# Weight sums by adding transfers in the plain token-stationary groups, with all signs turned to plus

## The chip, the cores and the metric

The kernel runs on one core of a Trainium2 chip. The time is device time in microseconds (us). TensorE (PE) multiplies, VectorE (DVE) and ScalarE (ACT) do elementwise work, GpSimd (POOL) does small arithmetic and issues transfers, SyncE (SP) issues transfers. All transfers of the core, whichever engine issues them, run on sixteen DMA engines.

## The reference

One block of a streaming encoder, 512 tokens of width 2048, all in float32:

```python
h = rms_norm(x, norm_g[l])
proj = h @ w_in[l]                       # 2048 -> 15,424 columns, split 13 ways
...
conv_y = b_gate * causal_depthwise_conv(c_gate * u, conv_w[l])
o_conv = (conv_y * jax.nn.silu(conv_z)) @ w_conv_out[l]
mla_y = mla_attention(c_q, c_kv, k_rope_raw, ...)      # 16 heads, block-causal
o_mla = (mla_y * jax.nn.silu(mla_z)) @ w_mla_out[l]
mem_y = memory_attention(mem_q, mem, ...)              # 4 heads over 256 memory tokens
o_mem = (mem_y * jax.nn.silu(mem_z)) @ w_mem_out[l]
merged = (jax.nn.sigmoid(g_conv) * o_conv + jax.nn.sigmoid(g_mla) * o_mla
          + jax.nn.sigmoid(g_mem) * o_mem)
x = x + merged @ w_o[l]
```

Most of the work is large matrix products with weights that are read once from memory.

## The kernel before, in words

**Products in three passes.** Every float32 operand is cut in two parts: ACT copies the raw tile to "whi" (the upper part), and DVE subtracts that from the raw tile and writes "wlo" (`forms_of`, by way of `split`). `mm3` makes a product of three matmuls: upper × upper, upper × lower, lower × upper.

**Seven products in place of eight.** Most of the large weight products are done as two-by-two block products: the tokens in two halves, the input width in two halves (tiles E and O), the output columns in two halves. With weight blocks w00, w01, w11, w10 (first digit: half of the input width; second: half of the columns), a group computes seven products P1 to P7. Each is a weight block, or a sum of weight blocks, times an activation block or a sum of such. P1, P4 and P2 use w00, w11 and w10 as they are. P7 uses w00 with w01, P5 uses w01 with w11, P6 uses P5's sum with w00, P3 uses P6's sum with w10. The sums of activations are made once by `build_sums`; the sums of weights are made in every group by DVE, in place, in the tile "raw" that holds the loaded block, and the result is cut into whi and wlo. The seven results are combined by `t_results` or `f_results` out of the accumulation banks X, Y, Z and W (`SLOT`).

**Three kinds of group.** A *feature-stationary* group (`f_group`, six of them) holds weights in PE and streams tokens. A *token-stationary* group (`t_group`, fifteen of them) holds tokens and streams 512 weight columns. Three of the fifteen are "lead" groups, the first after a change of activations, with an order of their own (`LEAD_ORDER`). The other twelve are called plain here: four for the conv branch (w_conv), five gate groups (one of w_gmem, two of w_gconv, two of w_gmla), w_memq, and the second groups of w_mla_out and w_o. There are also direct groups (`d_group`) without block sums.

**Steps.** A token-stationary group has 28 steps, one for each product and each of four chunks c of the input width. A step is made of forms (load, weight sum, whi and wlo) and parts (12 matmuls). `run_range` writes a step's matmuls, then the next step's forms, then what is to follow the step (results, loads of gates, transposes of the conv branch). whi and wlo lie in six buffers "wf", three steps' worth; in the attention stage some lie in "w" buffers. `T_ORDER` gives the order of steps of the plain groups:

```python
T_ORDER = [(n, c) for names in (("P1", "P7"), ("P5", "P4"), ("P6",), ("P3", "P2"))
           for c in range(4) for n in names]
```

**Loads.** All weight blocks stand in one list (`to_load`), 0.5 MB each as 128 × 1024 float32. `fetch(key)` issues loads on SP's queue up to that key, and beyond it up to eight ahead while fewer than `cap` of the ten "w" buffers are taken (`wlive`). `done(key)` gives a buffer back. A plain group before loads twenty blocks: 00 and 01 by turns, then 11, then 00 once more ("00b", for P6), then 10.

**Order on the engines.** SP's instructions run in the order of the program. In two stretches (the start, and the attention heads up to the first steps after them) the order on all engines is planned ahead by the kernel's own `Player`, with a table of costs. Elsewhere the framework's planner places the instructions of PE, DVE, ACT and POOL by an estimated timeline; each engine then takes its queue in that order.

**POOL.** In the first half POOL does next to nothing. In the mla_out groups (`mla_group`) POOL loads gates ("g", by `early`) and adds results into a tensor in memory ("mdram", by `store`, a transfer with accumulate); around it are loads of attention outputs ("araw") and of the conv groups' gates and sums ("g", "m"). In the w_o groups (`out_group`) POOL loads blocks of x and ACT's queue stores the output.

**Conv transposes.** After each pair of conv groups, `conv_turn` is hooked to steps 0, 2, 4 and 6 of the next plain group: eight PE transposes, three ACT and DVE passes each over 128 × 512.

Of the kernel before, what the change touches and what calls it, by code (L numbers as in the profile page):

```python
# [261 lines left out]
def body(ctx, tc, a, out):  # L262
# [142 lines left out]
    cap, limit = [NW], [None]  # L405

    def fetch(key):
        k = place[key]
        while issued[0] < len(loads) and (issued[0] <= k or (issued[0] < min(k + AHEAD, limit[0])
                                                             and wlive[0] < cap[0])):  # L410
            kk, src = loads[issued[0]]
            issued[0] += 1
            raws[kk] = w("raw")
            nc.sync.dma_start(flat(raws[kk]), src)
        return raws[key]

    def done(key):
        del raws[key]
        w_done()

    def to_load(key, src):
        place[key] = len(loads)
        loads.append((key, src))

# [17 lines left out]
    def run_all(gen):  # L442
        for _ in gen:
# [5 lines left out]
               for c in range(2) for n in names]  # L449
    T_ORDER = [(n, c) for names in (("P1", "P7"), ("P5", "P4"), ("P6",), ("P3", "P2"))  # L450
               for c in range(4) for n in names]
# [4 lines left out]
    def f_group(src, B, results, tag):  # L456
# [7 lines left out]
        def forms(name, c):  # L464
            w00, w01, w11, w10 = ((gid, k, c) for k in ("00", "01", "11", "10"))
            if name in ("P1", "P2", "P4"):
                key = {"P1": w00, "P2": w10, "P4": w11}[name]
                r = forms_of(fetch(key))
                if name != "P1":
                    done(key)  # L470
                return r
            if name == "P7":
                src_ = q("s")
                vec.tensor_tensor(out=src_, in0=fetch(w00), in1=fetch(w01), op=ALU.subtract)
                return forms_of(src_)
            i0, i1, op = {"P5": (w01, w11, ALU.add), "P6": (w01, w00, ALU.subtract),
                          "P3": (w10, w01, ALU.subtract)}[name]
            src_ = fetch(w01)
            vec.tensor_tensor(out=src_, in0=fetch(i0), in1=fetch(i1), op=op)
# [25 lines left out]
    def t_group(src, B, results, lead=False):  # L505
        gid = count[0] = count[0] + 1
        bk = {}
        w00, w01, w11, w10 = (src[4 * i:4 * i + 4] for i in range(4))
        cs_ = ((0, 1, 2), (3,)) if lead else ((0, 1, 2, 3),)
        for cs in cs_:  # L510
            if lead:
# [3 lines left out]
            else:  # L515
                for c in cs:
                    to_load((gid, "00", c), w00[c])
                    to_load((gid, "01", c), w01[c])
        for key, ws in ((("11b", w11),) if lead else (("11", w11), ("00b", w00))) + (("10", w10),):
            for c in range(4):  # L520
                to_load((gid, key, c), ws[c])

        def forms(name, c):
            key, other, op, dead = {
                "P1": ("00", None, None, ""), "P7": ("00", "01", ALU.subtract, "00"),
                "P5": ("01", "11", ALU.add, "11" if lead else ""),
                "P4": ("11b" if lead else "11", None, None, "11b" if lead else "11"),
                "P6": ("01", "00b", ALU.subtract, "00b"), "P2": ("10", None, None, "10"),
                "P3": ("01", "10", ALU.subtract, "01")}[name]
# [73 lines left out]
    def build_sums(E, O):  # L603
# [177 lines left out]
    def f_results(consume):  # L781
# [4 lines left out]
        def results(name, bk):  # L786
# [7 lines left out]
            elif name == "P5":  # L794
                vec.tensor_tensor(out=v, in0=bk["Z"], in1=v, op=ALU.add)
            elif name == "P6":
                vec.tensor_tensor(out=u, in0=bk["W"], in1=u, op=ALU.add)
                r1 = q("r1")
# [3 lines left out]
            elif name == "P3":  # L802
                sc["r0"] = q("r0")
                vec.tensor_tensor(out=sc["r0"][:, :, HS:], in0=pair(bk["Z"]), in1=pair(u), op=ALU.add)
# [11 lines left out]
    def t_results(put, direct, early=None, add=None, own=True):  # L816
# [4 lines left out]
        def results(name, bk):  # L821
            seen.add(name)
            if name in ("P1", "P7"):
                k, slot = ("u", "X") if name == "P1" else ("v", "Y")
                sc[k] = q(k)
                for tt in range(2):
                    act.activation(sc[k][:, tt], bk[slot][tt], AF.Copy)
                if early and name == "P7":
                    early(1, 1)
            u, v = sc.get("u"), sc.get("v")  # L830
            if name == "P5":
                for tt in range(2):
                    vec.tensor_tensor(out=v[:, tt], in0=bk["Z"][tt], in1=v[:, tt], op=ALU.add)
                if add:
                    vec.tensor_tensor(out=flat(v), in0=flat(v), in1=flat(add(1, 1)), op=ALU.add)
                if early:
                    early(0, 1)
# [8 lines left out]
            if name in ("P4", "P6") and seen >= {"P4", "P6"}:  # L846
# [3 lines left out]
                if add:  # L850
                    vec.tensor_tensor(out=flat(r), in0=flat(r), in1=flat(add(0, 1)), op=ALU.add)
                    vec.tensor_tensor(out=flat(u), in0=flat(u), in1=flat(add(1, 0)), op=ALU.add)
                put(0, 1, r)
# [4 lines left out]
            if name == "P3":  # L858
                r = q("r")
                for tt in range(2):  # L860
                    vec.tensor_tensor(out=r[:, tt], in0=bk["Z"][tt], in1=u[:, tt], op=ALU.add)
                put(1, 0, r)
# [859 lines left out]
```

## Time and profile before

| | |
|---|---|
| median of 3 runs | 2101.59 us (2100.2 to 2102.88) |
| profiled execution | 2101.8 us, span 2100.0 us |
| granted TensorE clock, mean | 0.998 |
| busy: PE, DVE, ACT, POOL | 99%, 78%, 50%, 7% |
| read from memory, written | 292.61 MB, 44.17 MB |
| queue of SP (q1) | 251.92 MB, 36.9% of sixteen engines' span |
| queue of POOL (q0) | 45.57 MB, 7.2% |

Busy time is the union of an engine's instructions. A line of groups reads: source line, engine, operation, result and operands, form, count, then busy time in us, mean in ns, and the idle time of the engine ahead of these instructions with what ended it. Nearly all work is recorded under line 233, where the kernel's recorder passes instructions on, so tiles' names tell the groups apart. A line of a stage reads: from and to, length, busy time of PE, weight loads, DVE, ACT and POOL with counts, granted clock, busy share of the DMA engines, GB/s.

### The profile page before, as it was taken

What the parts mean: (1) busy time and instruction counts of PE and PEld (TensorE: products, weight loads), DVE (VectorE), ACT (ScalarE), POOL (GpSimd) and SP (SyncE); (2) the same over time, 40 slices, a digit from 0 to 9 for tenths busy, and PEclk for the clock granted to TensorE, in tenths of its full rate; (3) what the DMA queues carried; (4) which work ended last, traced back from release to release, by engine and by line L of the source; (5) the groups of instructions that cost most, each with busy time, mean ns of one, the idle gap of its engine ahead of it and who ended that gap; (6) DMA issues with size and microseconds to landing.
All of it is one profiled execution on the core that took longest, in us unless ns stands there. A gap on an engine that the chain in (4) does not pass through costs nothing.

```text
span 2100.0 us, 28564 instructions
## 1 busy us (share of the span) xinstructions
PE 2083.3 (99%) x10818; PEld 1795.1 (85%) x10818; DVE 1642.5 (78%) x2162; ACT 1057.7 (50%) x1524; POOL 150.5 (7%) x183
## 2 busy tenths in 40 slices
PE   9999999999999999999999999999999999999999
PEld 9888888887899988899888888888988888888887
DVE  6887788788777787777787787788887688867987
ACT  5544344344444445444445566576776344433543
POOL 0000000000000000000000021213221201110000
PEclk9999999999999999999999999999999999999999
DMA  7346444444533445534546664312323867675672
GB/s 261 124 161 201 134 137 144 144 134 133 188 121 125 147 131 188 173 121 151 166 144 225 208 208 153 126 64 81 111 92 106 292 221 205 207 229 176 205 238 78
DMA packets 106332, 338.66 MB, mean 161 GB/s; under 512 B 11089, under 2 KB 11617, under 8 KB 106193
## 3 DMA queue, kind: packets, MB, share of 16 engines
q1 hardware_dynamic: 71360, 251.92, 36.9%
q0 software_dynamic: 13792, 45.57, 7.2%
q10 hardware_dynamic: 21040, 39.33, 5.0%
q8 instruction: 85, 1.39, 0.3%
q14 instruction: 55, 0.44, 0.1%
HBM read 292.61 MB, written 44.17 MB: 160 GB/s over the span
## 4 chain that ended last, share of the span: by engine, by line
PE 95%; DVE 2%; ACT 1%; issue 1%; DMA 1%; POOL 0%; ACTq 0%; DVEq 0%; POOLq 0%
PE aux L233 40%; PE acc L233 33%; PE aux L237 12%; PE acc L237 10%; DVE wlo L233 0%; DMA raw<-in_w_ckv 0%; DVE cv L233 0%; DVE raw L233 0%; ACT whi L233 0%; DMA raw<-in_w_mla_out 0%; DMA raw<-in_w_memz 0%; ACT s L237 0%; DVE ss L237 0%; DVE r L233 0%; DVE s L233 0%
## 5 line engine op out<-in xcount | busy, mean ns | idle before, releaser
L233 ACT ACTIVATE whi<-raw 128x1024 fp32r<-128x1024 f32 x521 | 550.5, 1060 | 765.2 <-PE aux L233 347.6
L233 DVE TENSOR_TENSOR wlo<-raw,whi 128x1024 fp32r<-128x1024 f32 x521 | 633.6, 1222 | 285.9 <-ACT whi L233 281.7
L233 DVE TENSOR_TENSOR raw<-raw 128x1024 f32<-128x1024 f32 x258 | 315.2, 1223 | 10.3 <-DMA raw<-in_w_mla_out 3.4
L233 PE MATMUL aux<-whi,b 128*128 128x512 f32 x896 | 293.3, 389 | 1.4 <-ACT whi L233 1.4
L233 PE MATMUL aux<-whi,f 128*128 128x512 f32 x880 | 289.7, 390 | 0.0
L233 PE MATMUL acc<-whi,b 128*128 128x512 f32 x880 | 287.1, 390 | 0.8 <-ACT whi L233 0.7
L233 PEld LDWEIGHTS aux<-whi,b 128*128 128x128 f32 x896 | 168.0, 188 | 37.0 <-ACT whi L233 2.3
L233 PEld LDWEIGHTS acc<-whi,b 128*128 128x128 f32 x880 | 164.9, 188 | 35.5 <-ACT whi L233 1.6
L233 PEld LDWEIGHTS aux<-whi,f 128*128 128x128 f32 x880 | 165.0, 188 | 34.3 <-ACT E L233 0.3
L233 PE MATMUL aux<-wlo,b 128*128 128x512 f32 x448 | 174.3, 389 | 0.0
L233 PE MATMUL aux<-wlo,f 128*128 128x512 f32 x440 | 171.9, 391 | 1.0 <-DVE wlo L233 0.9
L233 PE MATMUL acc<-wlo,b 128*128 128x512 f32 x440 | 171.8, 390 | 0.7 <-DVE wlo L233 0.7
L233 PE MATMUL acc<-whi,f 128*128 128x512 f32 x448 | 140.5, 389 | 0.0
L237 DVE TENSOR_TENSOR wlo<-raw,whi 128x1024 fp32r<-128x1024 f32 (+3 forms) x92 | 99.1, 1084 | 29.2 <-ACT whi L237 24.9
L237 ACT ACTIVATE whi<-raw 128x1024 fp32r<-128x1024 f32 (+3 forms) x92 | 86.6, 951 | 63.3 <-PE acc L237 23.0
L233 PEld LDWEIGHTS aux<-wlo,f 128*128 128x128 f32 x440 | 82.6, 188 | 19.4 <-DVE wlo L233 2.2
L233 PEld LDWEIGHTS aux<-wlo,b 128*128 128x128 f32 x448 | 84.1, 188 | 17.6 <-DVE wlo L233 0.2
L233 PEld LDWEIGHTS acc<-whi,f 128*128 128x128 f32 x448 | 84.1, 188 | 17.5
L233 PEld LDWEIGHTS acc<-wlo,b 128*128 128x128 f32 x440 | 82.6, 188 | 18.1 <-DVE wlo L233 1.2
L233 PE MATMUL acc<-wlo,f 128*128 128x512 f32 x224 | 87.1, 389 | 0.0
L233 PE MATMUL acc<-whi,mT 128*128 128x512 f32 x256 | 80.8, 392 | 0.0
L233 POOL DMA_DIRECT2D mraw<-in_memT x4 | 2.2, 552 | 1082.5 <-DMA gdram<-r 1061.2
(385 smaller groups left out, 4097.4 us busy)
## 6 DMA issues: line engine op xcount, KB each, us to landing
raw<-in_w_conv SPq DMA_DIRECT2D x80, 512.0 KB, 4.1
raw<-in_w_gmem SPq DMA_DIRECT2D x44, 512.0 KB, 3.9
raw<-in_w_mla_out SPq DMA_DIRECT2D x44, 512.0 KB, 5.1
raw<-in_w_o SPq DMA_DIRECT2D x44, 512.0 KB, 4.3
raw<-in_w_gconv SPq DMA_DIRECT2D x40, 512.0 KB, 4.0
raw<-in_w_gmla SPq DMA_DIRECT2D x40, 512.0 KB, 3.9
raw<-in_w_mlaz SPq DMA_DIRECT2D x32, 512.0 KB, 4.0
raw<-in_w_mem_kv SPq DMA_DIRECT2D x32, 512.0 KB, 4.8
```

The lines of the kernel that those rows point to most:

```text
L233: return f(*args, **kw)
L237: self.player.add(self.eng, lambda: f(*args, **kw), kind, writes, reads)
```

## The change

All weight sums become plain sums. `build_sums` turns the signs of two activation sums, and `f_results` and `t_results` turn additions into subtractions to match; the number of instructions there stays the same.

In the plain groups the sums for P5, P7 and P6 are no longer made by DVE. POOL's queue issues transfers that read a weight block from memory and add it to a raw tile in SBUF:

- w11 is added onto the tile of w01 (P5's sum). `to_load` carries it as `more`; `fetch` issues it once two further loads have been issued, or at the latest when the tile is fetched.
- When P1's forms of a chunk are made, w01 is added onto the tile of w00 (P7's sum).
- When P5's forms of a chunk are made, w00 is added onto the tile of w01 (P6's sum).

P3's sum stays with DVE. The second load of w00 goes, so a plain group has 16 loads and 12 adding transfers. The steps are put in the order P1, P5, P7, then P6 and P4 by turns, then P3 and P2 by turns. P5's result is the first that is copied from its banks, and P7's comes after it. Lead and feature-stationary groups keep their sums on DVE.

```diff
+    onto = []
+
     def fetch(key):
         k = place[key]
         while issued[0] < len(loads) and (issued[0] <= k or (issued[0] < min(k + AHEAD, limit[0])
                                                              and wlive[0] < cap[0])):
-            kk, src = loads[issued[0]]
+            kk, src, more = loads[issued[0]]
             issued[0] += 1
             raws[kk] = w("raw")
             nc.sync.dma_start(flat(raws[kk]), src)
+            if more is not None:
+                onto.append((kk, issued[0], more))
+            while onto and (issued[0] >= onto[0][1] + 2):
+                add_onto()
+        while any(kk == key for kk, _, _ in onto):
+            add_onto()
         return raws[key]
+
+    def add_onto():
+        kk, _, more = onto.pop(0)
+        nc.gpsimd.dma_start(flat(raws[kk]), more, accum_op=ALU.add)
...
-    T_ORDER = [(n, c) for names in (("P1", "P7"), ("P5", "P4"), ("P6",), ("P3", "P2"))
+    T_ORDER = [(n, c) for names in (("P1",), ("P5",), ("P7",), ("P6", "P4"), ("P3", "P2"))
                for c in range(4) for n in names]
...
+        else:
+            for c in range(4):
+                to_load((gid, "00", c), w00[c])
+            for c in range(4):
+                to_load((gid, "01", c), w01[c], w11[c])
+            for key, ws in (("11", w11), ("10", w10)):
+                for c in range(4):
+                    to_load((gid, key, c), ws[c])
 
         def forms(name, c):
-            key, other, op, dead = {
-                "P1": ("00", None, None, ""), "P7": ("00", "01", ALU.subtract, "00"),
...
+            key, other, dead = {
+                "P1": ("00", None, ""), "P7": ("00", "01", "00"), "P5": ("01", "11", "11" if lead else ""),
+                "P4": ("11b" if lead else "11", None, "11b" if lead else "11"),
+                "P6": ("01", "00b", "00b" if lead else ""), "P2": ("10", None, "10"),
+                "P3": ("01", "10", "01")}[name]
             src_ = fetch((gid, key, c))
-            if other:
-                ins = (src_, fetch((gid, other, c)))
-                in0, in1 = reversed(ins) if name == "P3" else ins
-                vec.tensor_tensor(out=src_, in0=in0, in1=in1, op=op)
+            if other and (lead or name == "P3"):
+                vec.tensor_tensor(out=src_, in0=src_, in1=fetch((gid, other, c)), op=ALU.add)
             r = forms_of(src_)
+            if not lead and name in ("P1", "P5"):
+                nc.gpsimd.dma_start(flat(src_), (w01 if name == "P1" else w00)[c], accum_op=ALU.add)
             for k in dead.split():
                 done((gid, k, c))
             return r
...
-        vec.tensor_tensor(out=v[0], in0=o1, in1=e1, op=ALU.subtract)
-        vec.tensor_tensor(out=v[1], in0=v[0], in1=e0, op=ALU.add)
+        vec.tensor_tensor(out=v[0], in0=e1, in1=o1, op=ALU.subtract)
+        vec.tensor_tensor(out=v[1], in0=e0, in1=v[0], op=ALU.subtract)
         vec.tensor_tensor(out=v[2], in0=o0, in1=v[1], op=ALU.subtract)
-        vec.tensor_tensor(out=e1, in0=e1, in1=e0, op=ALU.subtract)
+        vec.tensor_tensor(out=e1, in0=e0, in1=e1, op=ALU.subtract)
...
-            if name in ("P1", "P7"):
-                k, slot = ("u", "X") if name == "P1" else ("v", "Y")
-                sc[k] = q(k)
+            if name in ("P5", "P7"):
+                n, b = (1, bk["Z"]) if name == "P5" else (0, bk["Y"])
+                if "v" not in sc:
+                    sc["v"] = q("v")
+                    for tt in range(2):
+                        act.activation(sc["v"][:, tt], b[tt], AF.Copy)
+                    if early:
+                        early(1, 1)
+                else:
+                    v = sc["v"]
+                    for tt in range(2):
+                        ins = (b[tt], v[:, tt])
+                        vec.tensor_tensor(out=v[:, tt], in0=ins[n], in1=ins[1 - n], op=ALU.subtract)
...
+            if name == "P1":
+                sc["u"] = q("u")
                 for tt in range(2):
-                    act.activation(sc[k][:, tt], bk[slot][tt], AF.Copy)
-                if early and name == "P7":
-                    early(1, 1)
+                    act.activation(sc["u"][:, tt], bk["X"][tt], AF.Copy)
...
-                    vec.tensor_tensor(out=u[:, tt], in0=bk["W"][tt], in1=u[:, tt], op=ALU.add)
+                    vec.tensor_tensor(out=u[:, tt], in0=bk["W"][tt], in1=u[:, tt], op=ALU.subtract)
```

More of the change, by code (lines that the diff above doesn't have):

```diff
@@ L419, in done, with to_load @@
         w_done()
-    def to_load(key, src):
+    def to_load(key, src, more=None):
         place[key] = len(loads)
-        loads.append((key, src))
+        loads.append((key, src, more))
     class Step:
@@ L473, in forms @@
                 src_ = q("s")
-                vec.tensor_tensor(out=src_, in0=fetch(w00), in1=fetch(w01), op=ALU.subtract)
+                vec.tensor_tensor(out=src_, in0=fetch(w00), in1=fetch(w01), op=ALU.add)
                 return forms_of(src_)
-            i0, i1, op = {"P5": (w01, w11, ALU.add), "P6": (w01, w00, ALU.subtract),
-                          "P3": (w10, w01, ALU.subtract)}[name]
             src_ = fetch(w01)
-            vec.tensor_tensor(out=src_, in0=fetch(i0), in1=fetch(i1), op=op)
+            vec.tensor_tensor(out=src_, in0=src_, in1=fetch({"P5": w11, "P6": w00, "P3": w10}[name]), op=ALU.add)
             r = forms_of(src_)
@@ L508, in t_group @@
         w00, w01, w11, w10 = (src[4 * i:4 * i + 4] for i in range(4))
-        cs_ = ((0, 1, 2), (3,)) if lead else ((0, 1, 2, 3),)
-        for cs in cs_:
-            if lead:
+        if lead:
+            for cs in ((0, 1, 2), (3,)):
                 for key, ws in (("00", w00), ("01", w01), ("11", w11), ("00b", w00)):
@@ L514, in t_group @@
                         to_load((gid, key, c), ws[c])
[L515 to L519, printed above, removed]
-            for c in range(4):
-                to_load((gid, key, c), ws[c])
-        def forms(name, c):
-            key, other, op, dead = {
-                "P1": ("00", None, None, ""), "P7": ("00", "01", ALU.subtract, "00"),
[L526 to L529, printed above, removed]
+            for key, ws in (("11b", w11), ("10", w10)):
+                for c in range(4):
+                    to_load((gid, key, c), ws[c])
+        else:
+            for c in range(4):
+                to_load((gid, "00", c), w00[c])
[3 more added lines that the diff above has]
+                for c in range(4):
+                    to_load((gid, key, c), ws[c])
+        def forms(name, c):
+            key, other, dead = {
[3 more added lines that the diff above has]
+                "P3": ("01", "10", "01")}[name]
             src_ = fetch((gid, key, c))
-            if other:
-                ins = (src_, fetch((gid, other, c)))
-                in0, in1 = reversed(ins) if name == "P3" else ins
-                vec.tensor_tensor(out=src_, in0=in0, in1=in1, op=op)
+            if other and (lead or name == "P3"):
+                vec.tensor_tensor(out=src_, in0=src_, in1=fetch((gid, other, c)), op=ALU.add)
             r = forms_of(src_)
+            if not lead and name in ("P1", "P5"):
+                nc.gpsimd.dma_start(flat(src_), (w01 if name == "P1" else w00)[c], accum_op=ALU.add)
             for k in dead.split():
@@ L794, in results @@
             elif name == "P5":
-                vec.tensor_tensor(out=v, in0=bk["Z"], in1=v, op=ALU.add)
+                vec.tensor_tensor(out=v, in0=v, in1=bk["Z"], op=ALU.subtract)
             elif name == "P6":
-                vec.tensor_tensor(out=u, in0=bk["W"], in1=u, op=ALU.add)
+                vec.tensor_tensor(out=u, in0=bk["W"], in1=u, op=ALU.subtract)
                 r1 = q("r1")
@@ L803, in results @@
                 sc["r0"] = q("r0")
-                vec.tensor_tensor(out=sc["r0"][:, :, HS:], in0=pair(bk["Z"]), in1=pair(u), op=ALU.add)
+                vec.tensor_tensor(out=sc["r0"][:, :, HS:], in0=pair(bk["Z"]), in1=pair(u), op=ALU.subtract)
             elif name == "P2":
@@ L822, in results @@
             seen.add(name)
-            if name in ("P1", "P7"):
-                k, slot = ("u", "X") if name == "P1" else ("v", "Y")
-                sc[k] = q(k)
+            if name in ("P5", "P7"):
[11 more added lines that the diff above has]
+                        vec.tensor_tensor(out=v[:, tt], in0=ins[n], in1=ins[1 - n], op=ALU.subtract)
+                    if add:
+                        vec.tensor_tensor(out=flat(v), in0=flat(v), in1=flat(add(1, 1)), op=ALU.add)
+                    if early:
+                        early(0, 1)
+            if name == "P1":
+                sc["u"] = q("u")
                 for tt in range(2):
-                    act.activation(sc[k][:, tt], bk[slot][tt], AF.Copy)
-                if early and name == "P7":
-                    early(1, 1)
+                    act.activation(sc["u"][:, tt], bk["X"][tt], AF.Copy)
             u, v = sc.get("u"), sc.get("v")
[L831 to L837, printed above, removed]
             if name == "P6":
                 for tt in range(2):
-                    vec.tensor_tensor(out=u[:, tt], in0=bk["W"][tt], in1=u[:, tt], op=ALU.add)
+                    vec.tensor_tensor(out=u[:, tt], in0=bk["W"][tt], in1=u[:, tt], op=ALU.subtract)
                 r = q("r")
@@ L851, in results @@
                     vec.tensor_tensor(out=flat(r), in0=flat(r), in1=flat(add(0, 1)), op=ALU.add)
-                    vec.tensor_tensor(out=flat(u), in0=flat(u), in1=flat(add(1, 0)), op=ALU.add)
+                    vec.tensor_tensor(out=flat(u), in0=flat(u), in1=flat(add(1, 0)), op=ALU.subtract)
                 put(0, 1, r)
@@ L860, in results @@
                 for tt in range(2):
-                    vec.tensor_tensor(out=r[:, tt], in0=bk["Z"][tt], in1=u[:, tt], op=ALU.add)
+                    vec.tensor_tensor(out=r[:, tt], in0=bk["Z"][tt], in1=u[:, tt], op=ALU.subtract)
                 put(1, 0, r)
```

## The prediction

> **What bounds the kernel now.** I read the page first (busy time, slices, chain), then the chain in order of time, then the stages one by one.
>
> ```profile
> PE 2083.3 (99%) x10818; PEld 1795.1 (85%) x10818; DVE 1642.5 (78%) x2162; ACT 1057.7 (50%) x1524; POOL 150.5 (7%) x183
> PE   9999999999999999999999999999999999999999
> PE 95%; DVE 2%; ACT 1%; issue 1%; DMA 1%; POOL 0%; ACTq 0%; DVEq 0%; POOLq 0%
> ...
> L233 PE MATMUL aux<-whi,b 128*128 128x512 f32 x896 | 293.3, 389 | 1.4 <-ACT whi L233 1.4
> ...
> 200.37 24.48 PE aux L233 x108
> 224.85 10.88 PE acc L233 x48
> ```
>
> PE is busy for 99% of the span and in every slice. A busy PE need not be at its pace, so the chain in order of time is read for that: 108 matmuls of 512 columns in 24.48 us and 48 in 10.88 us, both 226.7 ns each, although one is shown as lasting 389 ns (they overlap). One step of a token-stationary group is 12 matmuls, 2.72 us; a group of 28 steps is 76.2 us. The change leaves the number of matmuls alone, so it can win only what PE loses against that pace in the twelve plain groups. These lie, by their loads, in 193–577 (four conv groups, one gate group), 737–891, 970–1198, about 1776–1852 and at the end.
>
> ```profile
> 192.00:268.00 76.00, 76.00 (x337) 62.90 (x337) 59.24 (x55) 30.73 (x31) 0.00 (x0) 1.00 0.43 134
> 344.00:422.00 78.00, 77.43 (x346) 63.37 (x345) 65.16 (x65) 32.63 (x36) 0.00 (x0) 1.00 0.46 148
> 500.00:577.00 77.00, 74.91 (x348) 61.53 (x346) 64.78 (x66) 38.35 (x43) 0.00 (x0) 1.00 0.50 164
> 1046.00:1122.00 76.00, 76.00 (x337) 62.94 (x336) 58.59 (x54) 35.80 (x38) 1.68 (x3) 1.00 0.53 178
> 1122.00:1198.00 76.00, 75.53 (x341) 62.40 (x340) 64.85 (x72) 44.27 (x56) 3.85 (x6) 1.00 0.57 190
> 1776.00:1852.00 76.00, 76.00 (x337) 62.94 (x336) 63.92 (x60) 35.26 (x36) 12.50 (x15) 1.00 0.75 229
> ```
>
> These are single groups: length, then busy time of PE, weight loads, DVE, ACT and POOL, clock, DMA share, GB/s. Undisturbed groups have PE at 76.00 of 76.00 with DVE at 59 us (78%): DVE is not late there. Three miss 0.57, 2.09 and 0.47 us, 3.1 us together. The first two carry the conv transposes, the third the memory tokens.
>
> ```profile
> PE aux L233 <- ACT whi L233: 1.4, 2, 1.0
> PE aux L233 <- DVE wlo L233: 0.9, 2, 0.5
> PE acc L233 <- DVE wlo L233: 0.8, 2, 0.4
> PE acc L233 <- ACT whi L233: 0.7, 1, 0.7
> ...
> L233 ACT ACTIVATE whi<-raw 128x1024 fp32r<-128x1024 f32 x25 | 26.5, 1059 | 34.4 <-PE aux L233 16.7 <-PE acc L233 9.5 <-DVE raw L233 8.1
> L233 DVE TENSOR_TENSOR raw<-raw 128x1024 f32<-128x1024 f32 x14 | 17.0, 1224 | 0.2
> ```
>
> Above are PE's waits from 190 to 1200 us; below, two groups of 500–577. ACT waited there 8.1 us for a weight sum (raw<-raw) on DVE. So the loss is DVE's: the sums share it with the conv arithmetic. Two of the seven waits (0.8 us) stand where a feature-stationary group begins, which keeps its DVE sums. The other five are 3.0 us, and each hides up to 389 − 227 ns more under a modelled end: 0.8 us. The ceiling of the gain is about 3.9 us.
>
> **The change, part by part.**
>
> *DVE sums.* A plain group had 16 sums (P7, P5, P6, P3, four each); P3's four stay. 12 × 12 = 144 go.
>
> ```profile
> L233 DVE TENSOR_TENSOR raw<-raw 128x1024 f32<-128x1024 f32 x258 | 315.2, 1223 | 10.3 <-DMA raw<-in_w_mla_out 3.4
> L233 DVE TENSOR_TENSOR wlo<-raw,whi 128x1024 fp32r<-128x1024 f32 x521 | 633.6, 1222 | 285.9 <-ACT whi L233 281.7
> raw<-in_w_conv SPq DMA_DIRECT2D x80, 512.0 KB, 4.1
> g<-gdram POOLq DMA_DIRECT2D x24, 512.0 KB, 7.1
> mdram<-r POOLq DMA_DIRECT2D x8, 512.0 KB, 9.3
> ...
> L233 POOL DMA_DIRECT2D mdram<-r x8: 1187/1240/1704, 1749.6 to 1853.8; - x8
> L233 POOL DMA_DIRECT2D m<-mdram x8: 724/724/1705, 1836.8 to 1926.4; - x8
> ...
> q0 software_dynamic: 575, 1.19, 86.4%
> q1 hardware_dynamic: 150, 0.55, 20.5%
> ```
>
> 144 × 1.223 = 176 us of DVE, 14.7 us of a group's 59. Nearly all of it lay beside PE. On the path it is worth between 0 and the 3.9 us above. In the new order the first eight steps (P1, P5) have no DVE sum, and there the conv transposes fall, so I take both of those losses as gone (4 waits, 2.6 us + 0.6 hidden) and half of the third: **−3.5 us**. The wait that follows next is PE's own pace.
>
> *Transfers.* A plain group goes from 20 loads on SP's queue to 16, and gains 12 adding transfers on POOL's: −48 and +144 over the program, 96 × 0.524 MB = 50 MB more read. The trace has no adding transfer into SBUF; the nearest row is mdram<-r, which adds into DRAM: 1.2 us of POOL to issue, 9.3 us to land. The last two rows are the queues from 1778.3 to 1785.9 us, where such adds filled q0: 1.19 MB at 86.4% of 7.6 us is 181 GB/s, against 0.55 MB at 20.5%, 353 GB/s, for loads. So half a megabyte costs all sixteen engines 2.9 us when added and 1.5 us when loaded. An add into SBUF may cost as little as a load (1.5) or as much as where the slowest one landed (13.6 us, below). I take 2.9 us and 9.3 us, the same operation.
>
> *DMA time of a group.* 20 × 0.524 MB in 76 us at share 0.43 is 1.6 us each. After: 16 × 1.6 + 12 × 2.9 = 60 us, 0.80 of 76, +0.37. Gate groups with stores come to 0.53 + 0.37 = 0.90. These fit. The mla_out group comes to 0.75 + 0.37 = 1.12: it does not.
>
> *The wait that is added.* A sum now has to land before ACT and DVE cut it into whi and wlo. "fetch" and the new order give the distances in steps: the add onto 00 follows P1 c and is needed by P7 c, 8 steps or 21.8 us on; the second onto 01 follows P5 c and is needed by P6 c, 8 to 11 steps on. The first one onto 01 is the tight one: it goes out once two later loads are issued, for c = 3 with the forms of step 2, and is needed by those of step 7, 5 steps or 13.6 us on. Behind it is slack: six wf buffers hold three steps, so forms begin two steps (5.4 us) ahead of PE and take 1.06 + 1.22 us, leaving 3.1. POOL is in order: ahead of that add stand the ones onto 00 c0, 01 c2 and 00 c1, released within two steps, 1.2 us of issue apart: 3 × 2.9 us of queue, of which 3.9 us have passed. So it lands after 9.3 + 4.8 = 14.1 us, against 13.6 − 1.2 + 3.1 = 15.5. It fits with 1.4 us to spare: **0**, in eleven groups. If the landing were the 13.6 us, it would be 2.9 us late; if an add took over 3.4 us of the engines, it would begin to be.
>
> [...]
>
> *mla_out's plain group.* Here POOL also adds results into mdram and loads gates.
>
> ```profile
> 1749.60 1.25 POOL L233 DMA_DIRECT2D mdram<-r  x1 [2.69 <-DVE r L233]
> 1760.60 0.74 POOL L233 DMA_DIRECT2D g<-gdram  x1 [9.75 <-DMA mdram<-r]
> 1774.72 1.20 POOL L233 DMA_DIRECT2D mdram<-r  x1 [12.13 <-DVE r L233]
> 1776.45 1.19 POOL L233 DMA_DIRECT2D mdram<-r  x1 [0.53 <-DVE r L233]
> 1787.24 0.72 POOL L233 DMA_DIRECT2D g<-gdram  x1 [2.29 <-DMA mdram<-r]
> 1795.04 0.72 POOL L233 DMA_DIRECT2D araw<-adram  x1 [4.72 <-PE aux L233]
> ...
> 1776.00:1796.00 20.00, 20.00 (x90) 16.57 (x89) 18.25 (x17) 10.23 (x12) 4.89 (x6) 1.00 0.99 274
> 1796.00:1816.00 20.00, 20.00 (x90) 16.57 (x89) 14.99 (x14) 7.68 (x9) 0.73 (x1) 1.00 0.73 252
> ...
> DMA to landing us min/median/max: 2.9/7.8/13.6
> ```
>
> POOL waits there for results and for landings (9.75 us once), and whatever adds stand behind wait too; the last line (landings on mdram) holds the 13.6. The first 40 us have 19.8 + 14.6 = 34.4 us of DMA already; twelve adds bring 34.8, and some 8 loads of 1.6, dropped or put off, take away 12.8: 56 us of work, through at 1832. The last add is needed by the forms of step 18, which begin at 1776 + 16 × 2.72 = 1820 and have 3.1 us of slack. So the bounds are 0 and 9 us late, once. Loads for later groups can slip further, so I take the lower part: **+3 us**.
>
> *The rest.* Signs in the sums of activations and results: same instructions, 0. Lead and feature-stationary groups: same counts, 0. P5's copy takes the place of P7's on ACT, 0. The kernel's tail keeps its order, 0. w_o's plain group:
>
> ```profile
> 2024.00:2100.00 76.00, 71.98 (x318) 59.28 (x316) 56.96 (x53) 28.62 (x29) 0.72 (x1) 1.00 0.34 119
> ...
> 2005.53 0.72 POOL L233 DMA_DIRECT2D x<-in_x  x1 [15.13 <-DMA out<-r]
> ```
>
> The engines of the DMA are light there (0.34), but an x load holds POOL's queue for 15 us just ahead of the group; the adds wait with it only if they are queued behind. I take 0; if they are, the second rival has the cost.
>
> *Sum.* Profiled execution 2101.8 us (span 2100.0): −3.5 + 3 gives 2101.3, less the 0.2 by which it stands above the median of 2101.59: **2101.1 us**. 0.2% (4.2 us) is about what a measurement of this kernel can tell from no change.
>
> **The rivals.** *Nothing is late (13%).* All of the PE losses go and mla_out loses nothing: 2101.6 − 3.9 = 2097.7, and with waits hidden under modelled ends 2097. For it: the queue drains after each burst, and loads after it can slip. Against: the 9.75 us wait on POOL. [...]
>
> *mla_out, or w_o, is late by more (13%).* 7 to 12 us in all in place of 3: 2105 to 2110. For it: share 0.99 already, and POOL's queue shared with stores that wait for DVE. Against: it is two groups of twelve, once each.
>
> *Slower: the add onto 01 c3 comes late in every plain group (15%).* From 3.4 us of engine time an add, or a landing above 10.7 us, PE stops at P5 c3. At the 13.6 us landing 2.9 × 11 = 32 us, 2130; at one third of that 2112. For it: only 1.4 us to spare, and gate groups at 0.90. Against: forms that come late also put off the later adds, so the queue empties.
>
> *It does not do what it says (2%)*: POOL's queue is laid out by a planner (araw went out at 1795, some 40 us ahead of its place in the program, six steps before the group's end); with an add behind such a load it could be late by tens of us.
>
> **How the numbers follow.** The forecast holds 57%: 2098 to 2105 by the bounds of its own terms. Faster by over 0.2% (under 2097.4) needs the whole ceiling and something hidden: 13%. Within: 58%, with the near ends of the rivals. Slower: 29%. The range of 8 in 10 reaches from 2097.2 to 2113, leaving out about 1 in 10 on each side.
>
> **What would show it.** DVE near 1466 us, raw<-raw near 114, HBM reads near 343 MB, POOL at some 150 + 144 × 1.2 = 320 us. In 500–577 and 344–422 PE's waits are gone; in mla_out's plain group PE waits for an ACT whose raw was waiting for a DMA of POOL's. Adds that land in under 12 us in the conv groups bear out the queue; PE waits in every plain group at P5 would prove it wrong, and so would a pace other than 226.7 ns.

## The result, and the profile after

The changed kernel takes 2126.32 us (median of 4 runs, 2123.66 to 2129.15); before, run beside it, takes 2101.69. The ratio is 1.0118 with a 95% interval of 1.0106 to 1.0130: slower, by 24.6 us. The forecast was 2101.1 us, its range 2097.2 to 2113.0. The profiled execution took 2129.15 us (span 2127.4), 2.8 above the median.

The page of the changed kernel, in the order of the parts that the prediction named (busy time, slices, chain, the sums, the queues):

```profile
PE 2089.7 (98%) x10818; PEld 1798.9 (85%) x10818; DVE 1481.0 (70%) x2018; ACT 1058.5 (50%) x1524; POOL 271.2 (13%) x327
PE   9999999999999999999998999999999999999998
...
q0 software_dynamic: 34528, 121.08, 25.1%
...
HBM read 342.94 MB, written 44.17 MB: 182 GB/s over the span
...
PE 89%; DMA 6%; DVE 2%; issue 1%; ACT 1%; POOL 0%; ACTq 0%; POOLq 0%; SPq 0%; DVEq 0%
...
L233 DVE TENSOR_TENSOR raw<-raw 128x1024 f32<-128x1024 f32 x116 | 141.8, 1224 | 28.3 <-DMA raw<-in_w_conv 6.5
...
raw<-in_w_conv SPq DMA_DIRECT2D x64, 512.0 KB, 5.2
raw<-in_w_conv POOLq DMA_DIRECT2D x48, 512.0 KB, 10.4
```

The edit did what it says. The sums on DVE fell from 258 to 116 under this line, DVE is busy 161 us less, 50 MB more are read. PE, which did the same 10818 matmuls, is no longer busy to the end of every slice, and the chain runs through DMA for 6% of the span where it was 1%. DVE now stands idle 28.3 us ahead of its own sums in place of 10.3; the largest share of it, 6.5 us, is for loads of w_conv.

The same windows as in the prediction, the first a microsecond later. The changed kernel falls behind by up to 11 us, so the later windows hold somewhat earlier steps (from and to, length, busy PE, weight loads, DVE, ACT, POOL, clock, DMA share, GB/s):

```profile
193.00:269.00 76.00, 74.55 (x329) 61.44 (x328) 46.55 (x44) 30.82 (x31) 9.39 (x11) 1.00 0.80 202
344.00:422.00 78.00, 76.00 (x345) 62.27 (x344) 52.91 (x55) 33.51 (x38) 8.55 (x10) 1.00 0.73 190
500.00:577.00 77.00, 71.78 (x325) 59.18 (x324) 49.42 (x51) 35.33 (x39) 4.28 (x5) 0.98 0.68 184
1122.00:1198.00 76.00, 67.83 (x285) 54.82 (x284) 43.46 (x47) 35.94 (x46) 12.40 (x16) 0.93 0.80 209
```

DVE is down from 59–65 us a group to 43–53, and yet PE misses 1.4, 2.0, 5.2 and 8.2 us where it missed 0, 0.6, 2.1 and 0.5. PE's waits name three causes (waited for, total, times, longest):

```profile
PE aux L233 <- ACT whi L233: 8.1, 1, 8.1
PE aux L233 <- DVE v L233: 7.6, 5, 1.7
PE aux L233 <- DVE cv L233: 6.0, 2, 4.7
```

**Place 1: P4's first step waits for a result (v).** The five waits lie at 218, 857, 1092, 1831 and 2080 us. The chain of the first, then DVE's timeline (start, length, instruction, idle time before it and its cause) and PE's:

```profile
206.02 1.24 DVE wlo L233
...
207.27 9.69 DMA raw<-in_w_conv
```
```profile
217.06 1.23 DVE L233 TENSOR_TENSOR raw<-raw 128x1024 f32<-128x1024 f32 x1 [4.37 <-DMA raw<-in_w_conv]
218.20 1.22 DVE L233 TENSOR_TENSOR wlo<-raw,whi 128x1024 fp32r<-128x1024 f32 x1
219.33 1.28 DVE L233 TENSOR_TENSOR v<-aux,v 128x512 f32<-128x512 f32 x2
...
220.17 0.47 PE L233 MATMUL aux<-whi,f 128*128 128x512 f32 x1 [1.45 <-DVE v L233]
```

The raw tile that DVE waits for at 217.06 is the first block of w10, for P3's sum, the one sum that was left on DVE. It is a plain load on SP's queue, issued at 207.27, and lands after 9.69 us. Queued behind that sum on DVE is "v", P7's result, and P4 needs the Y banks that v empties. Before, that result was a copy on ACT. Why the load is late is seen in three stretches ahead of it and in the landings:

```profile
185.00:195.00 10.00, 10.00 (x46) 8.28 (x45) 4.16 (x4) 4.73 (x5) 3.40 (x4) 1.00 1.06 251
195.00:205.00 10.00, 10.00 (x46) 8.29 (x45) 4.91 (x4) 4.44 (x7) 1.70 (x2) 1.00 1.06 223
205.00:215.00 10.00, 10.00 (x46) 8.29 (x45) 3.68 (x3) 4.66 (x5) 0.00 (x0) 1.00 1.05 281
...
L233 SPq DMA_DIRECT2D raw<-in_w_conv x4: 327/328/328, 201.8 to 210.0; - x4
...
DMA to landing us min/median/max: 7.7/9.0/9.7
```

Over the whole group the share is 0.80, as forecast; in its first half the DMA engines are full (1.05 to 1.06 up to 215 us): the twelve adds, issued from 171.8 to 199.4 us, are worked off there, and POOL's queue takes 80.4% of the engines from 185 to 215. The four loads of w10 that go out beside them land in 9.0 us (median); the same four land in 4.1 in e4, where the transfers do not add.

The waits at 857, 1092 and 2080 have the same rows ahead of them, a load of w10 that takes 7.9 to 9.9 us. The fourth, in mla_out's group, has another: its chain goes back to an add on POOL's queue, issued at 1806.70 for P6's last step, and ACT waits 1.7 to 2.7 us there for each of P6's four adds.

```profile
1806.70 23.47 DMA raw<-in_w_mla_out
```

**Place 2: the memory tokens' load.** The chain, then the landings of "mraw" (min/median/max), and stretches of 9 and 7 us:

```profile
1150.54 0.51 POOL raw L233
1151.04 18.77 DMA mraw<-in_memT
...
DMA to landing us min/median/max: 18.3/19.1/19.8
...
1164.00:1173.00 9.00, 0.86 (x3) 0.47 (x2) 2.17 (x5) 3.17 (x6) 0.00 (x0) 0.76 0.86 318
1173.00:1180.00 7.00, 6.96 (x19) 4.96 (x19) 6.33 (x11) 7.00 (x13) 0.00 (x0) 0.58 0.24 77
```

Before, these four loads were issued from 1107.5 to 1130.5 and landed in 3.9 to 6.8 us. Now POOL issues them from 1151 on, behind the group's adds, which go out one a step, and they land in 19.1. Between 1152 and 1160 plain loads go out on both queues, and the queue tells them apart (median us to landing):

```profile
mraw<-in_memT POOLq DMA_DIRECT2D x3, 512.0 KB, 19.4
raw<-in_w_gmla SPq DMA_DIRECT2D x3, 512.0 KB, 8.9
```

ACT waits 12.2 us for the first, with PE's next whi queued behind, and PE idles 8.1 us. Then PE runs for 7 us at a granted clock of 0.58, and loses another 7 × 0.42 = 2.9 us although it counts as busy. Together 11 us.

**Place 3: the conv transposes.** PE waits twice (4.7 and 1.3 us, up to 527 and 365) at the first matmul of a product for a bank that DVE's "cv" has still to read. Again the clock drops, to 0.76 from 525 to 532. Ahead of the shorter wait stands a store: ACT's queue sends the first cv to memory at 347.34, the store takes 7.35 us beside the adds (share 1.07 from 347 to 355; before, it took 2.0), and ACT waits for it before the next transpose's arithmetic.

```profile
354.77 0.72 ACT L233 ACTIVATE cv<-cu,gains 128x512 f32<-128x512 f32 x1 [6.97 <-DMA adram<-cv]
...
527.08 0.77 PE L233 MATMUL aux<-whi,f 128*128 128x512 f32 x1 [4.65 <-DVE cv L233]
```

**The sum.** Measured against 226.7 ns a matmul, the profiled execution has 27.3 us more excess than before's, and the span is 27.4 longer: memory tokens 11.0; P4's waits 7.6 and 5 × 0.16 hidden under modelled ends, 8.4; transposes 5.6; the first 25 us 2.0, where nothing is changed. These 2.0 us belong to this one execution: in e4's profile the same stretch takes as long as before's.

### The profile page after: what moved, and what is told of

The parts are those of the page before. It is cut to its first block, busy times and chain, and to the rows that moved or that the text cites. A ratio compares the mean times of both kernels' runs of the same rounds, so it can differ in the third digit from the quotient of the medians.

```text
span 2127.4 us, 28590 instructions
## 1 busy us (share of the span) xinstructions
PE 2089.7 (98%) x10818; PEld 1798.9 (85%) x10818; DVE 1481.0 (70%) x2018; ACT 1058.5 (50%) x1524; POOL 271.2 (13%) x327
## 3 DMA queue, kind: packets, MB, share of 16 engines
q0 software_dynamic: 34528, 121.08, 25.1%
HBM read 342.94 MB, written 44.17 MB: 182 GB/s over the span
## 4 chain that ended last, share of the span: by engine, by line
PE 89%; DMA 6%; DVE 2%; issue 1%; ACT 1%; POOL 0%; ACTq 0%; POOLq 0%; SPq 0%; DVEq 0%
PE aux L233 36%; PE acc L233 31%; PE aux L237 11%; PE acc L237 10%; DMA raw<-in_w_mla_out 2%; DMA mraw<-in_memT 1%; DVE wlo L233 1%; DMA raw<-in_w_gmla 1%; ACT whi L233 1%; DMA raw<-in_w_o 0%; DMA raw<-in_w_conv 0%; DMA raw<-in_w_gconv 0%; DMA adram<-cv 0%; POOL raw L233 0%; DMA xraw<-in_xT 0%
## 5 line engine op out<-in xcount | busy, mean ns | idle before, releaser
L233 PE MATMUL aux<-whi,b 128*128 128x512 f32 x896 | 288.2, 390 | 0.6 <-DVE r L233 0.6
L233 PE MATMUL acc<-whi,b 128*128 128x512 f32 x864 | 276.9, 390 | 0.1
L233 PEld LDWEIGHTS aux<-whi,f 128*128 128x128 f32 x896 | 169.9, 190 | 60.1 <-ACT whi L233 18.1
L233 DVE TENSOR_TENSOR raw<-raw 128x1024 f32<-128x1024 f32 x116 | 141.8, 1224 | 28.3 <-DMA raw<-in_w_conv 6.5
L233 PE MATMUL acc<-whi,f 128*128 128x512 f32 x448 | 146.5, 390 | 0.0
L237 POOL TENSOR_TENSOR rs_r<-rs_t,mhalf 128x4 f32<-128x4 f32 (+1 forms) x64 | 61.1, 957 | 186.2 <-DVE rs_t L237 165.8
## 6 DMA issues: line engine op xcount, KB each, us to landing
raw<-in_w_conv POOLq DMA_DIRECT2D x48, 512.0 KB, 10.4
```

Of the source, the lines that this page charges most:

```text
L233: return f(*args, **kw)
L237: self.player.add(self.eng, lambda: f(*args, **kw), kind, writes, reads)
```

## The experiments

Each edit is against the changed kernel, but for the last one; ratios are to before, run beside it.

| | us | ratio (95%) |
|---|---|---|
| e1_p4_late | 2117.65 | 1.0073 (1.0058–1.0088) |
| e2_turn_early | 2130.03 | 1.0134 (1.0119–1.0149) |
| e3_mraw_sp | 2117.92 | 1.0074 (1.0059–1.0089) |
| e4_plain_pool | 2102.95 | 1.0002 (0.9993–1.0012) |
| e5_no_p3_sum | 2118.14 | 1.0081 (1.0066–1.0096) |
| e6_dve_sums | 2125.04 | 1.0114 (1.0098–1.0129) |
| e7_p4_mraw | 2115.53 | 1.0068 (1.0053–1.0083) |
| e8_p4_mraw_turn | 2110.97 | 1.0048 (1.0032–1.0065) |
| e9_eight_adds | 2127.06 | 1.0119 (1.0102–1.0136) |
| e10_eight_turn_mraw | 2122.00 | 1.0094 (1.0079–1.0109) |
| e11_plain_turn | 2098.94 | 0.9988 (0.9979–0.9998) |
| e12_before_turn | 2105.40 | 1.0016 (1.0007–1.0025) |

Gains below are differences of these medians from the changed kernel's 2126.32 us. Reckoned from the before beside each run they come out 0.2 to 1.1 us larger or smaller, so about 1 us between two runs says nothing.

**P4 later (e1_p4_late).** P6's four steps come first, then P4's.

```diff
-("P7",), ("P6", "P4"), ("P3", "P2"))
+("P7",), ("P6",), ("P4",), ("P3", "P2"))
```

> Theory A (queue waits): the changed kernel loses 27 us of PE in its profile against before, in places, none of which is a late add: five times P4's first step waits 1.2 to 1.7 us for DVE to empty the Y banks (7.6 us in all, and some 0.16 us more each under modelled ends, 8.4 us). With P4 moved behind all four steps of P6 there are three more steps, 8 us, for that. A expects the five waits gone and 2126.3 - 8 = 2118 us. Theory B (the DMA engines are too full and the adds land late): P4 only looks like the place, its stall is passed on to P6 or P3; the time stays at 2124 to 2128.

8.7 us less. The waits for v are gone, and so is the one for the memory tokens' whi, although their load still lands after 18.5 us: with this order it is needed at another point. Of the twelve small waits for wlo, two stand in the kernel before as well. Among the new ones are three in mla_out's group, two in w_o's and one at 220 us at the steps of P6, which now follow one another without a P4 between them:

```profile
PE aux L233 <- DVE cv L233: 6.0, 2, 4.6
PE acc L233 <- DVE wlo L233: 5.4, 12, 0.7
```

In mla_out's group ACT waits there for adds (1.4 to 2.7 us each). At 220 us and in w_o's group it is the late load again: P3's first sum waits 4.2 and 4.5 us for it on DVE, and P6's wlo is queued behind. So place 1 is real, but without P4 the late transfers meet P6 instead, in waits of about half a microsecond.

**Transposes in steps 0 to 3 (e2_turn_early).**

```diff
-later.append((len(steps) + 2 * f, lambda h=h, f=f: conv_turn(h, f)))
+later.append((len(steps) + f, lambda h=h, f=f: conv_turn(h, f)))
```

> The conv transposes are hooked to steps 0, 1, 2, 3 in place of 0, 2, 4, 6. Theory A: in the changed kernel P5's banks are taken from step 4 and P7's from step 8, so a transpose of step 6 holds an aux bank that P7 needs, until DVE has multiplied it; PE waits 4.7 and 1.3 us for that. With the transposes through before P5 begins the two waits go: 2126.3 - 6 = 2120 us. A rival: DVE and ACT cannot do four transposes' work in four steps, and the wait moves to P5's forms (within 2 us of 2126). Theory B: no change, 2124 to 2128.

No gain, rather a loss. The long wait for cv is gone, but PE waits more elsewhere. In the second pair of conv groups it waits 3.2 us for r on DVE, which has the four hooks' arithmetic beside the forms. In the first pair ACT stands 5.9 us for the store of cv, which takes 7.4 us to land, and PE waits 2.0 us for whi and 1.3 for wlo right behind it. (A wait of 7.2 us for whi at 1172 is the memory tokens' again.) So the rival holds only in part: a store that lands late (2.0 us in before) has a hand in it.

**The memory tokens on SP's queue (e3_mraw_sp).**

```diff
-nc.gpsimd.dma_start(flat(mraw[j])...
+nc.sync.dma_start(flat(mraw[j])...
```

> The four loads of the memory tokens go on SP's queue in place of POOL's. Theory A: on POOL they stand behind the twelve adds of the gate group, are issued at 1151 us and take 18 to 20 us to land, ACT waits 12.2 us for the first and PE 8.1 us for ACT (11 us of PE in all in that stretch). On SP they land in 4 to 6 us: 2126.3 - 10 = 2116 us, and ACT's wait for mraw is gone. Theory B: the DMA engines are full there whatever the queue; the landing stays above 12 us and the time within 3 us of 2126.

8.4 us less; the load lands in 4.5 us and the wait of 8.1 is gone. Place 2 is worth about what was read from the trace (11), less what the next waits take. The edit changes two things, for on SP's queue the loads also go out later, from 1167.6 to 1178.8, when the adds are through (share 0.64 to 0.69). That the queue itself matters is seen in the changed kernel's two rows above, 19.4 against 8.9 us. The edit also moved waits elsewhere: two of the five for v became waits of 0.9 us for whi.

**The same transfers without adding (e4_plain_pool).** POOL's transfers overwrite; the same bytes, order and queue.

```diff
-nc.gpsimd.dma_start(flat(raws[kk]), more, accum_op=ALU.add)
+nc.gpsimd.dma_start(flat(raws[kk]), more)
...
-nc.gpsimd.dma_start(flat(src_), (w01 if name == "P1" else w00)[c], accum_op=ALU.add)
+nc.gpsimd.dma_start(flat(src_), (w01 if name == "P1" else w00)[c])
```

> All 144 transfers stay on POOL's queue, at their places, with the same bytes, but overwrite instead of adding (the weight sums of the plain groups are left out, but for P3's). Theory B: the engine time of an add (2.9 us against 1.5 of a load) is what costs, so most of the 24.7 us go: 2102 to 2108 us. Theory A: the waits come from the order in the queues and from banks; only the backlog of POOL's queue gets shorter, so the wait for the memory tokens shrinks (by 4 to 8 us) and the rest stays: 2118 to 2123 us.

Of PE's waits at the three places only the longer one for cv (4.7 us) is left: 23.4 us less, no difference from before. The one at 365 is gone with the late store: it lands in 3.25 us in place of 7.35. The rows that answer to places 1 and 2 (stretches, landings of the same four loads, queue and landings over the whole execution):

```profile
185.00:195.00 10.00, 10.00 (x45) 8.28 (x45) 4.89 (x4) 4.49 (x6) 1.92 (x4) 1.00 0.85 306
195.00:205.00 10.00, 10.00 (x45) 8.26 (x44) 4.65 (x4) 5.10 (x6) 0.73 (x2) 1.00 0.65 193
205.00:215.00 10.00, 10.00 (x46) 8.28 (x45) 6.54 (x8) 4.25 (x4) 0.00 (x0) 1.00 0.42 129
...
DMA to landing us min/median/max: 4.0/4.1/4.6
...
q0 software_dynamic: 34528, 121.08, 17.9%
...
raw<-in_w_conv POOLq DMA_DIRECT2D x48, 512.0 KB, 4.9
mraw<-in_memT POOLq DMA_DIRECT2D x4, 512.0 KB, 7.0
```

The same bytes on the same queue: with adding, q0's packets take 25.1% of 16 × 2127.4 us, without 17.9% of 16 × 2102.7. Less before's 7.2% of 16 × 2100.0, that is 6124 and 3603 engine-us for 144 transfers, 2.66 and 1.56 us of all sixteen engines each. This one difference, 1.1 us, moves the landing of these loads, P3's first among them, from 4.1 to 9.0 us and that of mraw from 7.0 to 19.1. (An add also holds POOL longer at its issue, 0.85 against 0.53 us.) The instructions on DVE and ACT, the order and the place of P7's result are the same in both kernels; alone they cost nothing at places 1 and 2. These need both the order and the full engines.

**No P3 sum (e5_no_p3_sum).** The four sums a group that DVE kept are left out; the blocks are loaded.

```diff
-if other and (lead or name == "P3"):
+if other and not lead and name == "P3":
+    fetch((gid, other, c))
+if other and lead:
```

> The changed kernel with P3's four weight sums left out in the plain groups (P3 multiplies P6's sum alone; P3's block is still loaded and fetched). Theory A now: the adds keep the DMA engines full for some 30 us of each group, a load behind them lands in 9 to 10 us in place of 4, the P3 sum that DVE has queued ahead of P7's result waits for that load, and P4 waits for P7's banks. Without the sum DVE has nothing to wait for there: P4's waits are gone with the steps where they were, 2126.3 - 8 = 2118 us. A rival: two steps are simply too few for DVE to empty the Y banks, sum or no sum; the waits of 1.2 to 1.7 us stay and the time is 2123 to 2127 us.

8.2 us less, and no wait for v is left. The adds are as many as before, so it is the sum, waiting for its load ahead of v on DVE, that carries the late load to PE. What remains is whi 7.6 and cv 6.0, places 2 and 3.

**The order with sums on DVE (e6_dve_sums).** Steps and signs stay as changed, no adding transfer, 24 loads a group.

```diff
-to_load((gid, "01", c), w01[c], w11[c])
+to_load((gid, "01", c), w01[c])
...
-if other and (lead or name == "P3"):
+if other and (lead or name != "P7"):
...
-if not lead and name in ("P1", "P5"):
-    nc.gpsimd.dma_start(flat(src_), (w01 if name == "P1" else w00)[c], accum_op=ALU.add)
+if not lead and name == "P1":
+    vec.tensor_tensor(out=src_, in0=src_, in1=fetch((gid, "01", c)), op=ALU.add)
```

> The new order of steps, signs and results, but no adds: the plain groups' sums are made by DVE again, with 24 loads a group (11 and 00 loaded twice more). It prices the order alone. Theory A (the order alone loses 4.7 us to the conv transposes' bank, as in the run with overwriting transfers, and nothing elsewhere): 2103 to 2108 us, with one PE wait for cv of 4 to 5 us and no waits for v. A rival: P4 one step behind P6's first is a bad order in itself, and with DVE fuller the waits for v are in all twelve groups: 2115 us or more.

This missed: as slow as the change itself, in the rival's range, but for neither reason given. No wait for v appears; it is the transposes.

```profile
PE aux L233 <- DVE cv L233: 15.2, 4, 6.1
PE aux L233 <- DVE wlo L233: 2.8, 2, 2.2
```

The new order is worse for the transposes, a little with DVE relieved (e4) and much more with its sums back: P5 and P7 take the aux banks from steps 4 and 8, and the transposes hang on steps 0 to 6. With DVE's sums in between, cv comes later still.

**Two and three cures (e7_p4_mraw, e8_p4_mraw_turn).** e7 joins e1 and e3. e8 adds, from e7, transposes at steps 0, 1, 3 and 5.

```diff
-later.append((len(steps) + 2 * f, lambda h=h, f=f: conv_turn(h, f)))
+later.append((len(steps) + (0, 1, 3, 5)[f], lambda h=h, f=f: conv_turn(h, f)))
```

> P4 behind all of P6, and the memory tokens' loads on SP's queue. If the two losses are separate places (theory A) their gains add: 2126.3 - 8.7 - 8.4 = 2109 us. If P4's move had already helped the memory tokens (its profile showed no long wait there), the second edit brings little: 2114 to 2118 us.

> As the run with P4 behind P6 and the loads on SP's queue, and the conv transposes hooked to steps 0, 1, 3 and 5 in place of 0, 2, 4 and 6. Theory A: the last transpose's bank is then free before P7 takes it at step 8 and the 4.7 and 1.3 us waits shrink: 4 to 6 us under the run without this edit. The rival, from the run with steps 0 to 3 (4 us slower than the changed kernel): ACT and DVE are short there whichever the step, and it is within 2 us of the run without it or slower.

e7 gains 10.8 us on the change, not 8.7 + 8.4, and is not clearly better than e1, which had already taken PE off the late memory tokens. e8 gains 4.6 more, as expected for place 3. What it still waits for:

```profile
PE acc L233 <- DVE wlo L233: 5.1, 11, 0.7
PE aux L233 <- DVE cv L233: 2.6, 3, 1.3
```

Eight of the eleven stand at steps of P6, seven of these from the gate group at 1159 us on. The three in mla_out's group start at 1806.12, 1809.82 and 1813.31 us, 3.5 to 3.7 us apart in place of 2.72: ACT waits there 1.4 to 2.7 us a time for a tile of w_mla_out to land, and PE cannot go faster than the adds. The other five stand behind the late load: at 1157 and 2059 us DVE waits 4.6 and 4.5 us for it ahead of P3's first sum, with P6's wlo queued behind.

**Eight adds in place of twelve (e9_eight_adds, e10_eight_turn_mraw).** P6's sum goes back to DVE, with w00 loaded again; e10 adds e8's transposes and e3's queue.

```diff
-for key, ws in (("11", w11), ("10", w10)):
+for key, ws in (("11", w11), ("00b", w00), ("10", w10)):
...
-if other and (lead or name == "P3"):
+if other and (lead or name in ("P3", "P6")):
...
-if not lead and name in ("P1", "P5"):
-    nc.gpsimd.dma_start(flat(src_), (w01 if name == "P1" else w00)[c], accum_op=ALU.add)
+if not lead and name == "P1":
+    nc.gpsimd.dma_start(flat(src_), w01[c], accum_op=ALU.add)
```

> P6's sum goes back to DVE, with w00 loaded again: 8 adds and 20 loads in a plain group in place of 12 and 16. By the runs an add takes 2.7 us of all DMA engines and a load 1.6, so the group needs 53 us of them in place of 58, and the burst behind P1 and P5 is four adds (11 us) shorter. If the time that the burst takes from the loads behind it sets the loss: the memory tokens' load lands in time, P3's first load too; 2126.3 - 16 = 2110 us (2106 to 2114), the conv transposes' waits staying. If the loss came with DVE's place in the order (the run with all sums on DVE had 2125 us): 2122 us or more.

> As the run with eight adds, with the conv transposes at steps 0, 1, 3 and 5 and the memory tokens' loads on SP's queue. If both edits bring what they did beside twelve adds (4.5 and up to 8 us, the second perhaps nothing where the burst is shorter): 2103 to 2106 us, still not under the kernel before. A rival: with DVE making P6's sum the transposes' arithmetic is late again: 2110 us or more.

Both missed the first figure and lie in the rival's range. A third fewer adds gains nothing. The load of mraw still takes 15.5 us in e9, but ACT no longer waits for it. In its place cv's waits grow to 8.4 us, and PE waits for wlo 8.5 us in all. The two longest of these (3.3 and 2.2 us) stand behind a weight sum on DVE that waits for its load:

```profile
1824.29 1.23 DVE L233 TENSOR_TENSOR raw<-raw 128x1024 f32<-128x1024 f32 x1 [2.82 <-DMA raw<-in_w_mla_out]
```

So P6's sum, back on DVE, is one more instruction that waits there for a load with other work queued behind it. (The two loads take 6.8 and 3.5 us to land, and in the chain each goes out only when DVE has ended an earlier instruction, probably because a buffer comes free with it; that was not tested.) e10 wins back 5 us and keeps the waits for wlo, with the same row ahead of the longest (2.5 us of waiting for a load at 1820). Why cv's waits are longer than in the change was not settled.

**The ceiling (e11_plain_turn).** e4 with transposes at 0, 1, 3 and 5.

> As the run with overwriting transfers on POOL (sums left out but for P3's), with the conv transposes at steps 0, 1, 3 and 5. It is the ceiling of the idea, adds as cheap as loads and no bank wait: 2103.0 - 4.5 = 2098.5 us, 0.15% under the kernel before. If ACT and DVE are short there whichever the step, it stays at 2103.

2098.94 us, 2.6 below before beside it (0.9988). With DVE relieved and transfers at the price of loads, the waits that the prediction wanted gone are nearly gone:

```profile
PE aux L233 <- DVE cv L233: 1.7, 2, 1.2
PE acc L233 <- DVE wlo L233: 0.8, 2, 0.4
PE aux L233 <- DVE r L233: 0.7, 2, 0.6
```

**The transposes' steps in the kernel before (e12_before_turn).** The edit of e8, in before.

> The kernel before, with the conv transposes hooked to steps 0, 1, 3 and 5: does the one edit that paid beside the adds pay without them? Before, the transposes' groups lose some 4.5 us. If the bank of the last transpose has a part in it: 2099 to 2100 us, 0.1% under before. If it is only DVE's sums between the transposes (what the profile of before showed), moving them closer together makes it slower: 2102 to 2106 us.

3.8 us slower than before. So the gain from e4 to e11 (4.0 us, or 2.8 from the befores beside them) is not in the steps as such. In the old order the sums on DVE seem to stand in the way of transposes at 1, 3 and 5: PE waits 2.9 us for wlo in place of 0.9, and 1.7 for whi in place of 1.4.

No kernel with adding transfers reached before's time; the best, e8, is 9.7 us above before beside it.

## Why the prediction was wrong

**What held.** DVE 1481 us (forecast near 1466), raw<-raw 116 (114), HBM reads 342.94 MB (343). The price of an add on the engines was 2.66 us (taken 2.9), its landing in the conv groups 10.4 us (taken 9.3), a group's share 0.80 (0.80). POOL was below the forecast (271 against 320): the issue took 0.85 us, not 1.2. And the wait to which the prediction gave most room, the first add onto 01 with c = 3, before P5's forms, did not come: PE waits at P5 once, 0.6 us at 358, and that is behind the conv transposes. The term **0** for eleven groups ("It fits with 1.4 us to spare") was right as it stood.

**Where it failed.** The step is *DMA time of a group*, at "0.80 of 76 … These fit". It averaged over a group what is issued in its first half. From 185 to 215 us the engines are full at 1.06, and the group's second half pays for it only in an average. Having found that the adds themselves arrive in time, the prediction charged nothing to the other transfers that share the engines ("loads after it can slip" stands in it as a point in favour): P3's load (4.1 to 9.0 us), mraw (5.8 to 19.1) and a store of cv (2.0 to 7.35). e4 shows it: the same order at 1.56 us a transfer has none of the waits behind these three.

**The rest costed at nothing.** "P5's copy takes the place of P7's on ACT, 0" and "Signs … same instructions, 0" counted instructions and not their queue. P7's result moved from ACT to DVE, behind a sum that waits for a load and ahead of P4, which wants the same banks: 8.4 us (e5 removes this wait alone and gains 8.2). And POOL's queue was followed for araw, g, m and x, but not for mraw, a few steps after the adds of a gate group: 11 us (e3 gains 8.4).

**The gain.** "−3.5 us" assumed that no sum in the first eight steps meant no wait for the transposes. The order also hands the aux banks on earlier, and the late store of cv adds its part: the transposes cost 5.6 us more, not 3.2 less. That the wait of 4.7 us is for the banks is the reading of its place; e4, where it stays, and e6, e8 and e11 agree with it, but no run isolated a bank. The size was near: e11, with the order mended and the transfers cheap, gains 2.6 of the 3.9 us of ceiling.

**mla_out.** The +3 us had the right mechanism and nearly the right size. Its twelve adds are the slowest in landing (18.4 us), P6's forms wait for them, and PE loses 1.65 us in the group, at P4, to a v that is queued behind the last of these forms and P3's first sum. In e1 and e8, where P6 runs unbroken, PE meets the adds directly. w_o's group, taken as 0, has a v wait as well, behind a late load.

**The rivals.** The third one, slower by an add that is late in every plain group, had the right size (2112 to 2130) and the wrong place: what is late is a load on SP's queue beside the adds, in four groups, in mla_out's an add itself, and once a load queued behind the adds on POOL. Its chance of 15% was low because its price was tied to one wait instead of to the full engines.

## What to carry to other kernels

When a transfer that is dear in engine time (here 2.66 against 1.56 us of all sixteen) takes over work from a compute engine, draw the share of the DMA engines over the stretch in which it is issued, not over the group, and then ask of every other load and store in that stretch, on any queue, what stands behind it. An instruction that moves to another engine costs nothing only if nothing ahead of it in its new queue waits (P7's result, moved to DVE, came to 8.4 us); look up what is queued there and who needs its result. And the gain of freeing an engine that is not the bound was known beforehand (3.9 us): a change with so low a ceiling can carry hardly any risk.

## What the runs showed of the hardware

**An add into SBUF cost 1.7 times the plain transfer** of the same half megabyte on the same queue (2.66 us of all sixteen engines in the changed kernel, 1.56 in e4), and landed in 10.4 instead of 4.9 us (median) in the conv groups, where twelve follow one another.

**Two stalls of PE cost more than their length.** After 8.1 us of idling the granted clock was 0.58 over 7 us, and a matmul of 512 columns took some 0.43 us, not 0.227:

```profile
1172.54 1.22 PE L233 MATMUL aux<-whi,f 128*128 128x512 f32 x2 [8.13 <-ACT whi L233]
...
1176.52 1.05 PE L233 MATMUL aux<-whi,f 128*128 128x512 f32 x2
1177.38 0.63 PE L233 MATMUL aux<-wlo,f 128*128 128x512 f32 x1
1177.80 0.63 PE L233 MATMUL aux<-whi,f 128*128 128x512 f32 x1
```

From 1176.52 to 1177.38 there are two matmuls, 0.43 us each. The clock was 0.50 up to 1178 and 0.55 from 1178 to 1179, so it was back some 6.4 us into the work. After the 4.7 us (work from 527.08) it was 0.50 up to 530 and 0.82 from 530 to 531, back some 3.3 us into the work. Behind the five waits of up to 1.7 us for v it stayed at 1.00. The length of a wait alone does not tell these apart: in the same profile a wait of 2.1 us up to 11.69 was followed by 0.50 from 12 to 14, and in before, at the attention heads, one of 1.8 us up to 1375.65 by 0.50 from 1376 to 1379. The prediction had no such term: before's waits in its plain groups are of at most 1.0 us, and its clock is 1.00 in all the windows of them that the prediction shows.
